# A modulation vector of 48 columns computed in three places instead of one

## The chip, the cores and the metric

The kernel runs on one core of one Trainium2 chip. The metric is the device time of one execution in microseconds (us); of several runs the median is given. One core has five engines with a queue of instructions each: TensorE (PE in the profile, with its weight loads as PEld), VectorE (DVE), ScalarE (ACT), GpSimd (POOL) and SyncE (SP), which here issues most DMAs. An engine works its queue off in order and waits where an operand or a buffer is not ready.

## The reference, cut to what matters

The input x has 512 tokens of 1024 features. It passes two blocks with different weights. The change lies in the second, whose norms and residual sums are modulated by a vector c of 1024 elements:

```python
c_act = jax.nn.silu(c)
mod = (c_act @ w_mod[l] + b_mod[l])[:, None, :]          # w_mod: 1024 x 6144
sh1, sc1, g1, sh2, sc2, g2 = jnp.split(mod, N_MOD, axis=-1)

h = _rms(x, norm1_w[l]) * (1 + sc1) + sh1
proj = h @ w_in[l]
...                                                      # S5 branch, sliding-window attention
x = x + g1 * (mixed @ w_out[l])

h2 = _rms(x, norm2_w[l]) * (1 + sc2) + sh2
x = x + g2 * _conv_ffn(h2, w_up[l], conv_w[l], conv_b[l], w_down[l])
```

The product with w_mod is one row by a matrix of 25 MB in fp32; its 6144 results are held as `modT`, 48 columns of 128 partitions. Columns 0 to 7 are the shift and 8 to 15 the scale of the first norm, 16 to 23 the gate g1, 24 to 31 and 32 to 39 shift and scale of the second norm, 40 to 47 the gate g2.

## The kernel before, in words

Feature tiles of 128 partitions by 512 tokens are the unit of work. In the trace the stages follow one another: block 1 (projections, three kinds of attention, a convolution, an output projection) to about 318 us, its feed-forward stage ("first feed-forward stage", weights w3 and w4) to about 722 us, the second block (S5 state space branch, sliding-window attention, gated linear unit, output projection) to about 955 us, and the "second feed-forward stage" (w8 and w9) to the end.

Weights come as pieces of 128x1024 fp32 (512 KB) over one queue, `_Lazy`: SP loads a piece into `raw` (L353; NRAW = 2 buffers), ACT rounds it to `whi` (L365), DVE or, for w6 to w8, POOL forms the rest `wlo` (L367), and PE multiplies with both parts (helper `mm`, L259). A `raw` buffer comes free when `wlo` is formed. One piece is prepared ahead of the one in use (AHEAD = 1).

In the feed-forward stages PE's products go to banks of `acc`; DVE empties them (`fg` L1299 and `fu` L1302 for the hidden tiles, `x` L1323 for the sum), which frees the bank for PE. Two generators of second-block work are interleaved with the first feed-forward stage: `s5_tables` and `modulation` (L1052). The function `fill()` (L1225) steps each generator once after every finished tile of that stage. `modulation` holds silu(c), spread over all partitions, in `cb`, and computes each of the 48 columns in two halves: SP loads 128x512 of w_mod into `wm` (three buffers, 256 KB), and one DVE instruction (L1061) multiplies it with `cb` and sums along the row. Whatever is left of the generators is run before the second block's first norm. The column groups of `modT` are read by `modulated` (both norms, through `a1`), `gm` (g1) and `down2` (g2, L1705).

ACT's functions come in table sets; a function outside the loaded set needs an ACT_TABLE_LOAD ahead of it. `tables()` at L306 loads a set by name that holds both the logarithm and the exponential, since `rsqrt_` (L497) writes every inverse square root as exp(-0.5 ln). In block 1 the head norms use it: `nss` (sums of squares on DVE), `nr` by L498 and L499 on ACT, a Newton step on DVE, `tokn`, and PE's transposes of `tokn`.

The order of PE's instructions in the second block is written out by hand in the string ORDER (a name and a number for each step: s, t and v are the three parts of the attention of one tile, g the gated unit, p the output products of the S5 branch, qp and qt projections and transposes of the queries, R and A norms). Elsewhere, and on the other engines everywhere, a scheduler sets the order at build time by its own estimate of when operands are ready; code that is written earlier and depends on little may be moved far ahead.

Of the kernel before, what the change touches and what calls it, by code (L numbers as in the profile page):

```python
# [17 lines left out]
P = 128  # L18
# [20 lines left out]
B2 = 1  # L39
# [6 lines left out]
ORDER = "U kp0 kp1 a0 a1 kt0 b0 qp0 c0 a2 b1 qp1 kt1 b2 c1 d0 a3 c2 qt0 qt1 b3 c3 d1 s0 qp2 s1 s2 t0 d2 t1 d3 e0 s3 e1 qt2 t2 s4 qp3 v0 t3 s5 v1 g0 qt3 g1 g2 t4 g3 s6 v2 v3 s7 t5 R p0 p1 v4 p2 t6 v5 p3 p4 v6 t7 p5 v7 p6 p7 A"  # L46
# [17 lines left out]
# ------------------------------------------------------------------ layout  # L64
# [29 lines left out]
def w_plan():  # L94
    """name -> list of (input, row0, n_k, columns): one contiguous [128, n_k * n] block each."""
# [29 lines left out]
def pvec(i):  # L125
    """per-partition vectors, name -> [128, n]"""
# [17 lines left out]
    o["b_mod"] = _fv(z(i["b_mod_2"])[0])  # L144
    o["sinks"] = _bc(z(i["sinks_2"])[0])
# [17 lines left out]
def consts():  # L163
    """constants of the shapes alone, name -> [128, n]"""
# [36 lines left out]
def arrays_of(i):  # L201
# [15 lines left out]
    a["wmod"] = np.ascontiguousarray(g("w_mod_2")[0].T).reshape(48, P, D)  # L217
    br, bi = (g(f"ssm_b_{n}_2")[0].transpose(1, 0, 2).reshape(64, 512) for n in ("re", "im"))
# [11 lines left out]
# ------------------------------------------------------------------ kernel  # L230
def build(tc, I, out, PV, PVN, CS, CSN, CS1, CSN1):
# [52 lines left out]
    # ---- constants and per-partition vectors  # L284
# [18 lines left out]
    def tables(after=None, name="natural_log_exp_and_others"):  # L303
        """activation tables that the next functions share"""
# [8 lines left out]
    # ---- weights: load, split into two 12-bit parts whose sum is the weight  # L313
# [10 lines left out]
    def cut(name, j):  # L324
        """block j as pieces: (first k, last k, first column, last column) each, with its source"""
# [11 lines left out]
    class _Lazy:  # L337
# [80 lines left out]
    for name, n in ( ("w2", 4), (("w3", "w4"), 0), ("w5", 5), ("w6", 2), ("w7", 8), (("w8", "w9"), 0)):  # L418
        if n == 0:
            enqueue_ffn(*name)  # L420
        for j in range(n):
# [21 lines left out]
    def proj_f(ps, w, x, m, k0=0, cs=ALL):  # L443
        """ps[m-feature, token] = W[:, m].T @ x"""
# [4 lines left out]
    def proj_group(group, x, order, cs=ALL):  # L449
        """several (ps, w, m) at once, the contraction outermost"""  # L450
# [6 lines left out]
    def proj_late(ws, x, early, late, done):  # L457
        """all 8 feature tiles; the first three wait for the late part of x last"""
# [13 lines left out]
    def proj_t(ps, w, x, t, n, o=0):  # L472
        """ps[token, o:o + n] = x[:, token].T @ W"""
# [13 lines left out]
    def split_scaled(dst, src, scale_col):  # L487
        """dst hi/lo of src * scale_col"""
# [7 lines left out]
    def rsqrt_(o, ms, scale=1.0):  # L496
        """o = (ms * scale + eps) ** -0.5, from the tables"""  # L497
# [3 lines left out]
    def rsqrt_m2(pool, tag, r, ms):  # L501
        """r = -2 * (ms + eps) ** -0.5, with a Newton step"""
# [6 lines left out]
    def head_norm(pool, wide, dsts, src, nh):  # L509
        """dsts[i][tok, heads, dup, 64] = -128 * src[tok, heads, 64] / rms, the heads in order"""  # L510
# [19 lines left out]
    # gains with the factors that the norms leave open: -1/128 per head norm, -1/2 per feature norm  # L530
# [12 lines left out]
    # ================================================================ block 1  # L543
# [6 lines left out]
    # ---- x, its squares, the unscaled normed input; the first products run along as the tiles of x come in  # L550
# [50 lines left out]
    # ---- bias tables of the causal attentions  # L601
# [11 lines left out]
    # compress chain inputs  # L613
# [11 lines left out]
    # ---- keys, values and gates of the sparse attention; queries and keys of all heads  # L625
# [15 lines left out]
    def kv_p(n):  # L641
        """two query tiles at a time"""
# [28 lines left out]
    def turn2(src):  # L671
        """both query tiles of a pair of heads side by side"""
# [6 lines left out]
    def kv_x(n):  # L679
        """hi and lo of the keys, the same on both halves of the partitions"""  # L680
# [12 lines left out]
    def qa_x(t):  # L693
        """the hi part of the queries on the lower half of the partitions, the lo part on the upper half"""
# [31 lines left out]
    # ---- compressed keys and values  # L726
# [65 lines left out]
    # ---- compressed branch, all tiles at once  # L792
# [28 lines left out]
    # ---- group norm of a finished feature tile, split for the next product  # L821
# [20 lines left out]
    # ---- softmax of one query tile, 4 heads  # L842
# [58 lines left out]
    # ---- stick-breaking: what is left of the stick before a key is the product of 1 - sigmoid over the later keys  # L901
# [32 lines left out]
    # ---- dilated  # L934
# [24 lines left out]
    # ---- short convolution  # L959
# [43 lines left out]
    def tok_norm(pool, parts, r, w="onesD", cs=ALL):  # L1003
        """-2 / rms of every token, on all partitions; the parts add up to the squares"""
# [26 lines left out]
    # ---------------------------------------------------------------- feed-forward 1, with work of block 2 beside it  # L1031
# [19 lines left out]
    def modulation():  # L1051
        cb = s5p.tile([P, D], F32, name="cb")  # L1052
        nc.sync.dma_start(cb, I["cbc"])
        act(cb, cb, AF.Silu)
        mh = s5p.tile([P, 2, 48], F32, name="mh")
        yield
        for j in range(48):
            for n in range(2):
                wm = s5p.tile([P, 512], F32, tag="wm", bufs=3, name="wm")
                nc.sync.dma_start(wm, I["wmod"][j][:, n * 512:(n + 1) * 512])  # L1060
                V.tensor_tensor_reduce(wm, wm, cb[:, n * 512:(n + 1) * 512], 1.0, 0.0, ALU.mult, ALU.add, mh[:, n, j:j + 1])  # L1061
            yield
        V.tensor_tensor(modT, mh[:, 0], mh[:, 1], op=ALU.add)
        V.tensor_tensor(modT, modT, V1("b_mod"), op=ALU.add)
        dbg("mod", modT)
        yield

    def s5_tables():
# [3 lines left out]
        def cmul(o_r, o_i, a_r, a_i, b_r, b_i, shape, E):  # L1072
            """o = a * b, complex; o may not overlap a or b"""
# [41 lines left out]
        # (a - 1) / lambda  # L1115
# [17 lines left out]
        # mag ** 8 and the rotations of 8, 16, .. 256 steps  # L1133
# [14 lines left out]
        for q in range(4):  # L1148
# [16 lines left out]
            # input to the state at the end of a chunk of 8 tokens  # L1165
# [17 lines left out]
            # state to output, powers 0..8  # L1183
# [11 lines left out]
            # within a chunk  # L1195
# [15 lines left out]
            # rotations of 0..63 chunks  # L1211
# [11 lines left out]
    fillers = [s5_tables(), modulation()]  # L1223
# [42 lines left out]
    def norm_tail(pool, tot, r, after, hold, before=None, TAIL=TAIL, NPOS=NPOS):  # L1266
        """the last feature tiles by halves of the tokens: the norm of one half runs beside the products of the other"""
# [42 lines left out]
    def sum_squares(tot, k, src, cs, sq):  # L1310
        """adds to tot, except for the last one, which is returned"""
# [36 lines left out]
    def start_u(cs):  # L1348
        if cs is HALVES[0]:
# [17 lines left out]
    # ================================================================ block 2  # L1367
# [373 lines left out]
```

## Time and profile before

| | |
|---|---|
| median of 3 runs | 1321.94 us (1320.47 to 1323.9) |
| the profiled execution's own time (span) | 1323.2 us |
| PE busy | 1247.0 us, 94% |
| DVE busy | 864.9 us, 65% |
| ACT busy | 501.5 us, 38% |
| POOL busy | 386.4 us, 29% |
| share of PE in the chain that ended last | 53% |
| share of DVE, of DMA | 16%, 8% |

The rows further down come from the profile of that one execution. Line numbers such as L1061 are those of the kernel before. The granted clock of TensorE (PEclk) is 1.00 at 2.4 GHz and 0.50 at 1.2 GHz; values between are means over a stretch.

### The profile page before, as it was taken

To read this page: it belongs to the slowest core of one execution; us is meant where nothing else is said; L and a number is where in the kernel's file an instruction comes from. 1 tells how busy PE (TensorE), PEld (TensorE's weight loads), DVE (VectorE), ACT (ScalarE), POOL (GpSimd) and SP (SyncE) were. 2 spreads that over 40 slices of the span, in tenths; PEclk is the share of its full clock that TensorE was granted. 3 is DMA by queue.
4 is the path that set the end of the run, shared out by engine and by line. 5 is a ranking of instruction groups with operands and counts; after the bars stand their busy time and mean duration, and the time that the engine had idled before them with its cause. 6 is when DMAs were issued, how large, how long until landed. Compare 5 with 4: busy or idle time off the path is not lost.

```text
span 1323.2 us, 17207 instructions
## 1 busy us (share of the span) xinstructions
PE 1247.0 (94%) x6269; PEld 1005.0 (76%) x6269; DVE 864.9 (65%) x1615; ACT 501.5 (38%) x862; POOL 386.4 (29%) x403
## 2 busy tenths in 40 slices
PE   7999999999979878999999989979899999999998
PEld 6888765667857657788888978757888888888887
DVE  7668768767988878745445778795855443435362
ACT  5334466445213122322233432663454333333330
POOL 3000004012327439092511143025152423232300
PEclk8999999999999999999999986779899999999999
DMA  5431111126567676643434763331132423232321
GB/s 213 140 123 49 50 32 49 51 77 197 160 198 252 196 248 200 187 147 111 145 109 156 268 175 116 80 96 58 39 99 84 135 85 107 82 108 82 105 87 63
DMA packets 163668, 164.11 MB, mean 124 GB/s; under 512 B 12160, under 2 KB 127760, under 8 KB 163584
## 3 DMA queue, kind: packets, MB, share of 16 engines
q1 hardware_dynamic: 154240, 146.43, 36.2%
q0 software_dynamic: 4256, 12.29, 3.0%
q10 hardware_dynamic: 5088, 4.29, 1.0%
q8 instruction: 49, 0.80, 0.3%
q14 instruction: 35, 0.29, 0.1%
HBM read 149.39 MB, written 15.43 MB: 125 GB/s over the span
## 4 chain that ended last, share of the span: by engine, by line
PE 53%; DVE 16%; DMA 8%; issue 4%; ACT 2%; POOL 0%; DVEq 0%; SPq 0%; ACTq 0%; POOLq 0%
PE acc L259 31%; PE sc L259 10%; PE tr L259 9%; DMA wm<-in_wmod_dram 6%; DVE wm L1061 3%; DMA raw<-in_w_dram 2%; DVE wlo L367 2%; PE po L259 1%; ACT whi L365 1%; DVE hd L494 1%; DVE z L1441 1%; DVE x L1655 1%; DVE z L1442 1%; PE tr L1591 0%; DVE sqsum L1317 0%
## 5 line engine op out<-in xcount | busy, mean ns | idle before, releaser
L259 PE MATMUL acc<-hl,whi 128*128 128x512 f32 (+1 forms) x1624 | 489.5, 385 | 20.9 <-DVE fg L1299 7.5
L259 PEld LDWEIGHTS acc<-hl,whi 128*128 128x128 f32 x1624 | 298.8, 192 | 90.3 <-issue 19.1
L365 ACT ACTIVATE whi<-raw 128x1024 fp32r<-128x1024 f32 (+1 forms) x187 | 193.9, 1039 | 378.4 <-PE acc L259 178.0
L259 PE MATMUL acc<-hl,wlo 128*128 128x512 f32 (+1 forms) x812 | 311.2, 383 | 0.0
L367 DVE TENSOR_TENSOR wlo<-raw,whi 128x1024 fp32r<-128x1024 f32 (+1 forms) x133 | 170.3, 1282 | 67.4 <-ACT whi L365 64.7
L367 POOL TENSOR_TENSOR wlo<-raw,whi 128x1024 fp32r<-128x1024 f32 x54 | 132.2, 2450 | 265.9 <-ACT whi L365 265.9
L259 PEld LDWEIGHTS acc<-hl,wlo 128*128 128x128 f32 x812 | 155.1, 191 | 32.3 <-issue 2.4
L259 PE MATMUL acc<-hd,whi 128*128 128x512 f32 (+1 forms) x472 | 146.4, 393 | 19.3 <-DVE fu L1302 9.2
L259 PEld LDWEIGHTS acc<-hd,whi 128*128 128x128 f32 x472 | 87.9, 191 | 42.7 <-issue 12.7
L259 PE MATMUL acc<-whi,hl 128*128 128x256 f32 (+1 forms) x544 | 111.2, 295 | 1.6 <-ACT tok L246 1.6
L1061 DVE CUSTOM_DVE_ANT_0 wm<-wm,cb 128x512 f32<-128x512 f32 x96 | 87.1, 929 | 30.3 <-DMA wm<-in_wmod_dram 29.3
L259 PEld LDWEIGHTS acc<-whi,hl 128*128 128x128 f32 x544 | 91.1, 199 | 6.2 <-ACT tok L246 3.0
L259 PE MATMUL acc<-hd,wlo 128*128 128x512 f32 (+1 forms) x236 | 92.5, 392 | 0.0
L259 PE MATMUL acc<-wlo,hl 128*128 128x256 f32 (+1 forms) x272 | 79.9, 294 | 0.5 <-DVE wlo L367 0.5
L259 PE MATMUL tr<-hl,whi 128*128 128x512 f32 (+1 forms) x240 | 72.8, 386 | 0.0
L259 PE MATMUL sc<-hl,whi 128*128 128x512 f32 x208 | 64.9, 393 | 0.0
L914 POOL TENSOR_SCALAR_AFFINE_SELECT keep<-keep 128x128 f32<-128x128 f32 x16 | 9.3, 595 | 185.2 <-ACT keep L908 184.4
L259 PEld LDWEIGHTS acc<-wlo,hl 128*128 128x128 f32 x272 | 54.3, 200 | 2.6 <-DVE wlo L367 1.0
L259 PEld LDWEIGHTS acc<-hd,wlo 128*128 128x128 f32 x236 | 45.3, 192 | 9.5
L259 PEld LDWEIGHTS tr<-hl,whi 128*128 128x128 f32 x240 | 44.5, 188 | 9.8
L1323 DVE TENSOR_TENSOR x<-x,acc 128x512 f32<-128x512 f32 (+1 forms) x49 | 31.9, 655 | 28.8 <-PE acc L259 28.7
L259 PE MATMUL tr<-hl,wlo 128*128 128x512 f32 (+1 forms) x120 | 46.3, 386 | 0.0
(422 smaller groups left out, 1963.8 us busy)
## 6 DMA issues: line engine op xcount, KB each, us to landing
raw<-in_w_dram SPq DMA_DIRECT2D x177, 512.0 KB, 4.3
wm<-in_wmod_dram SPq DMA_DIRECT2D x96, 256.0 KB, 3.9
xk<-in_xT_dram SPq DMA_DIRECT2D x16, 256.0 KB, 4.7
d_g<-s5g POOLq DMA_DIRECT2D x4, 576.0 KB, 4.3
gt<-d_g SPq DMA_DIRECT2D x4, 576.0 KB, 4.0
w1c<-in_w1k_dram SPq DMA_DIRECT2D x8, 256.0 KB, 5.7
w1c<-in_w1v_dram SPq DMA_DIRECT2D x8, 256.0 KB, 7.1
raw<-in_w_dram SPq DMA_DIRECT2D x8, 256.0 KB, 2.7
```

What stands on the lines that cost most here:

```text
L259: nc.tensor.matmul(o, lhsT=l, rhs=r, start=start, stop=stop, **k)
L365: act(hi[:, :m], raw[:, :m], AF.Copy)
L367: E.tensor_tensor(lo[:, :m], raw[:, :m], hi.bitcast(F32)[:, :m], op=ALU.subtract)
L494: V.tensor_tensor(dst[:, 1], src, dst.bitcast(F32)[:, 0], op=ALU.subtract)
L914: G.affine_select(g[:, d], g[:, d], fill=1.0, **past)
L1061: V.tensor_tensor_reduce(wm, wm, cb[:, n * 512:(n + 1) * 512], 1.0, 0.0, ALU.mult, ALU.add, mh[:, n, j:j + 1])
L1323: V.tensor_tensor(x[k][:, cs], x[k][:, cs], ps[:, cs], op=ALU.add)
L1441: V.scalar_tensor_tensor(dst[re], src[im], sign, t[im], op0=ALU.mult, op1=ALU.mult)
L1442: V.scalar_tensor_tensor(dst[im], src[re], -sign, t[re], op0=ALU.mult, op1=ALU.mult)
L1655: V.tensor_tensor(x[k][:, cs], x[k][:, cs], t[:, cs], op=ALU.add)
```

## The change

The 48 columns are computed in three places.

- Columns 0 to 23 stay in the first feed-forward stage, by the same DVE instruction. The generator takes two or three steps of `fill()` for a column (`wait`), where it took one.
- Columns 24 to 39 become sixteen steps m24 to m39 in ORDER, in the second block. Each loads 128x1024 of a re-ordered copy of w_mod, `wmodk`, through the weight queue into a `raw` buffer (`_ModPiece`), multiplies it in eight fp32 products of one column with silu(c) (`cT`, features on the partitions) into a bank of the `tr` pool, and DVE adds b_mod. The 16 pieces stand among those of w6 and w7 in the queue, in order of use.
- Columns 40 to 47 are computed by DVE in the second feed-forward stage, into a tile `modG`, stepped after each of its tiles.

`cT` is computed by one Silu on ACT from a column group of `pv`, which gets 8 more columns. The factors of the two norms (`norm_gain`) are formed separately, those of the second norm after m39. Docstrings and comments also go away.

```diff
+MOD1, MOD2 = 24, 40
-ORDER = "... s4 qp3 v0 t3 s5 v1 g0 qt3 g1 g2 t4 g3 s6 v2 v3 s7 t5 R p0 p1 v4 p2 t6 v5 p3 p4 v6 t7 p5 v7 p6 p7 A"
+ORDER = "... s4 qp3 m24 v0 m25 t3 m26 s5 v1 m27 g0 m28 qt3 m29 g1 m30 g2 m31 t4 g3 m32 s6 m33 v2 v3 m34 s7 t5 m35 R p0 m36 p1 v4 m37 p2 t6 m38 v5 p3 p4 m39 v6 t7 p5 v7 p6 p7 A"
...
+    class _ModPiece(_Lazy):
+        def fetch(self):
+            if self.raw is None:
+                self.raw = wpool.tile([P, WM], F32, tag="raw", bufs=NRAW, name="raw")
+                nc.sync.dma_start(self.raw[:, :D], I["wmodk"][self.j])
+        def load(self):
+            self.fetch()
+            self.parts = self.raw
...
-    def modulation():
+    def modulation(pool, j0, j1, dst, wait):
...
-            yield
+            for _ in range(wait(j)):
+                yield
...
+    act(cT, V1("c"), AF.Silu)
...
-    fillers = [s5_tables(), modulation()]
+    fillers = [s5_tables(), modulation(s5p, 0, MOD1, modT[:, :MOD1], lambda j: 2 + j % 2)]
...
+    def mod_p(j):
+        w = wpieces["mod", j].get()
+        ps = tr()
+        for k in range(KD):
+            mm(ps[:, :1], w[:, k * P:(k + 1) * P], cT[:, k:k + 1], k == 0, k == KD - 1)
+        V.tensor_tensor(modT[:, j:j + 1], ps[:, :1], V1("b_mod", j), op=ALU.add)
+        if j == MOD2 - 1:
+            norm_gain(1)
...
-        V.scalar_tensor_tensor(x[k], ps, modT[:, 40 + k:41 + k], x[k], op0=ALU.mult, op1=ALU.add)
+        V.scalar_tensor_tensor(x[k], ps, modG[:, k:k + 1], x[k], op0=ALU.mult, op1=ALU.add)
...
+    last8 = modulation(fp, MOD2, 48, modG, lambda j: j % 2)
-    ffn("w8", "w9", h2, hidden2, down2, start=started, banks=(tr, sc, acc) if B2 else (acc,))
+    ffn("w8", "w9", h2, hidden2, down2, lambda: next(last8, None), start=started, banks=(tr, sc, acc) if B2 else (acc,))
```

What this does to the order of instructions shows at three places. The first is ACT's queue at the start of block 1. The names: `hl` is a tile of x in two parts, `pv` the vectors, `nr` the inverse root of a head norm. Before, its first rows, and further down the first head norm:

```order
L306 ACT_TABLE_LOAD
L623 DMA w2c<-in_w2c_dram 128x256
L489 ACTIVATE hl<-xk,pv 128x512
...
L365 ACTIVATE whi<-raw 128x1024
L498 ACTIVATE nr<-nss,eps 128x4
L499 ACTIVATE nr<-nr 128x4
L246 ACTIVATE tok<-sc,r_tok 128x128
```

With the change, the same places on ACT:

```order
L309 ACT_TABLE_LOAD
L647 DMA w2c<-in_w2c_dram 128x256
L1097 ACT_TABLE_LOAD
L1097 ACTIVATE cT<-pv 128x8
L513 ACTIVATE hl<-xk,pv 128x512
...
L522 ACT_TABLE_LOAD
L522 ACTIVATE nr<-nss,eps 128x4
L523 ACT_TABLE_LOAD
L523 ACTIVATE nr<-nr 128x4
L249 ACTIVATE tok<-sc,r_tok 128x128
```

The Silu of `cT`, written at the start of the feed-forward stage, has moved to ACT's first work of the program, behind the load by name. From there to about 230 us of the trace the logarithm and the exponential of each norm of block 1 have a load each: the program has 45 ACT_TABLE_LOADs instead of 18, one for `cT` and 13 pairs more.

The second place is PE in the second block, behind the last projection of the queries (qp3). `po` is an attention output, `prob` the weights of it, `sc` the scores. Before:

```order
L259 MATMUL acc<-whi,hl 128x256
L259 MATMUL po<-pt,v_6746 64x2x128 x2
L1591 MATMUL tr<-cst,prob_7590 128x128 x8
L259 MATMUL sc<-k2T_6748,q2T_6751 128x256
L259 MATMUL sc<-k2T_6748,q2T_6752 128x256
```

With the change, the same place on PE:

```order
L262 MATMUL acc<-whi,hl 128x256
L262 MATMUL tr<-cT,raw 128x1 x8
L262 MATMUL po<-pt,v_6603 64x2x128 x2
L262 MATMUL tr<-cT,raw 128x1 x8
L1625 MATMUL tr<-cst,prob_7443 128x128 x8
L262 MATMUL tr<-cT,raw 128x1 x8
L262 MATMUL sc<-k2T_6605,q2T_6608 128x256
```

Sixteen such groups of eight products now stand in PE's order between the steps of the attention, the gated unit and the output products.

The third place is SP's queue in that part of the second block, where `x_4` to `x_7` are the residual tiles read back. Before:

```order
L1637 DMA x_3_8095<-d_x 128x512
L353 DMA raw<-in_w_dram 128x1024 x2
L1637 DMA x_4_8119<-d_x 128x512
L353 DMA raw<-in_w_dram 128x1024
L1637 DMA x_5_8156<-d_x 128x512
```

With the change, the same place on SP:

```order
L1681 DMA x_3_8132<-d_x 128x512
L381 DMA raw<-in_wmodk_dram 128x1024 x2
L356 DMA raw<-in_w_dram 128x1024
L381 DMA raw<-in_wmodk_dram 128x1024 x3
L356 DMA raw<-in_w_dram 128x1024
L1681 DMA x_4_8152<-d_x 128x512
L381 DMA raw<-in_wmodk_dram 128x1024
L1681 DMA x_5_8207<-d_x 128x512
```

The pieces of w6 and w7 now alternate with pieces of `wmodk`, all of them in the two `raw` buffers.

## Rows read from the trace of the kernel before

**Rows 1.** The page: busy time by engine, and the chain that ended last.

```profile
PE 1247.0 (94%) x6269; PEld 1005.0 (76%) x6269; DVE 864.9 (65%) x1615; ACT 501.5 (38%) x862; POOL 386.4 (29%) x403
...
PE 53%; DVE 16%; DMA 8%; issue 4%; ACT 2%; POOL 0%; DVEq 0%; SPq 0%; ACTq 0%; POOLq 0%
```

**Rows 2.** The page: groups (busy, mean ns | idle before), DMA issues (KB, us).

```profile
L365 ACT ACTIVATE whi<-raw 128x1024 fp32r<-128x1024 f32 (+1 forms) x187 | 193.9, 1039 | 378.4 <-PE acc L259 178.0
...
L367 POOL TENSOR_TENSOR wlo<-raw,whi 128x1024 fp32r<-128x1024 f32 x54 | 132.2, 2450 | 265.9 <-ACT whi L365 265.9
...
L1061 DVE CUSTOM_DVE_ANT_0 wm<-wm,cb 128x512 f32<-128x512 f32 x96 | 87.1, 929 | 30.3 <-DMA wm<-in_wmod_dram 29.3
...
raw<-in_w_dram SPq DMA_DIRECT2D x177, 512.0 KB, 4.3
```

**Rows 3.** Stretches: length, busy time of the engines, clock, DMA share, GB/s.

```profile
core 0: us, PE busy (x) PEld busy (x) DVE busy (x) ACT busy (x) POOL busy (x), PEclk, DMA share, GB/s
317.00:432.00 115.00, 104.57 (x450) 82.89 (x449) 100.95 (x256) 35.47 (x50) 49.82 (x61) 0.96 0.66 205
432.00:541.00 109.00, 92.15 (x386) 71.33 (x385) 88.94 (x143) 22.49 (x30) 58.05 (x74) 0.95 0.69 216
...
566.00:700.00 134.00, 134.00 (x610) 108.22 (x609) 65.71 (x74) 39.30 (x51) 57.19 (x108) 1.00 0.41 123
...
853.60:906.90 53.30, 44.53 (x211) 32.41 (x209) 42.38 (x85) 31.92 (x76) 18.36 (x9) 0.87 0.23 70
960.00:1300.00 340.00, 340.00 (x1511) 277.91 (x1510) 157.99 (x205) 125.59 (x158) 99.47 (x41) 1.00 0.32 95
```

**Rows 4.** Waits: PE's from 432 to 541, then one of DVE's, 300 to 722.

```profile
PE acc L259 <- DVE fg L1299: 8.8, 3, 4.0
PE acc L259 <- DVE x L1323: 5.7, 4, 2.7
...
DVE wm L1061 <- DMA wm<-in_wmod_dram: 29.3, 25, 3.0
```

**Rows 5.** Timeline of PE (start, us): fp32 products of 64 columns, of one.

```profile
829.86 0.39 PE L259 MATMUL acc<-sp,gt 128*128 128x64 f32 x2
...
831.20 0.39 PE L259 MATMUL acc<-sp,gt 128*128 128x64 f32 x2
...
794.08 0.63 PE L259 MATMUL acc<-ua,tt 128*128 128x64 f32 x2
...
799.63 0.64 PE L259 MATMUL acc<-sp,gt 128*128 128x64 f32 x2
...
25.85 1.33 PE L259 MATMUL tr<-cst,sqs 128*128 128x1 f32 x8
```

**Rows 6.** Stretches as in Rows 3, and PE's waits from 853.6 to 906.9.

```profile
794.00:813.40 19.40, 17.94 (x84) 17.38 (x84) 16.85 (x36) 3.05 (x8) 7.74 (x6) 0.50 0.27 85
828.70:831.50 2.80, 2.80 (x27) 2.80 (x27) 2.38 (x10) 2.76 (x4) 0.00 (x0) 1.00 0.00 0
...
860.00:884.00 24.00, 15.25 (x71) 11.14 (x69) 22.59 (x31) 14.16 (x27) 9.92 (x4) 0.84 0.41 121
...
PE sc L259 <- DVE ml L1573: 4.9, 1, 4.9
PE tr L1524 <- DVE pt L248: 3.8, 1, 3.8
```

**Rows 7.** Timeline of ACT: a change of table sets, two head norms; PE's transpose.

```profile
230.08 1.28 ACT L498 ACT_TABLE_LOAD   x1
231.37 0.69 ACT L498 ACTIVATE rg<-sc,eps 128x512 f32<-128x512 f32 x1
...
39.72 0.30 ACT L498 ACTIVATE nr<-nss,eps 128x4 f32<-128x4 f32 x1 [2.07 <-DVE nss L515]
...
43.55 0.29 ACT L498 ACTIVATE nr<-nss,eps 128x4 f32<-128x4 f32 x1
...
45.99 0.66 PE L676 MATMUL tr<-cst,tokn 128*128 128x128 f32 x4 [0.28 <-DVE tokn L526]
```

More of the change, by code (lines that the diff above doesn't have):

```diff
@@ L45 @@
 EN_AT = {'k1': (0, 4), 'v1': (4, 4), 'q1': (8, 12), 'h1': (20, 8), 'w1': (28, 8), 's1': (36, 8), 'o1': (44, 16), 't1': (60, 46), 'u2': (106, 4), 'z2': (110, 4), 'y2': (114, 4), 'k2': (118, 2), 'v2': (120, 2), 'q2': (122, 4), 'h2': (126, 12), 's2': (138, 12), 't2': (150, 14)}
-ORDER = "U kp0 kp1 a0 a1 kt0 b0 qp0 c0 a2 b1 qp1 kt1 b2 c1 d0 a3 c2 qt0 qt1 b3 c3 d1 s0 qp2 s1 s2 t0 d2 t1 d3 e0 s3 e1 qt2 t2 s4 qp3 v0 t3 s5 v1 g0 qt3 g1 g2 t4 g3 s6 v2 v3 s7 t5 R p0 p1 v4 p2 t6 v5 p3 p4 v6 t7 p5 v7 p6 p7 A"
+ORDER = "U kp0 kp1 a0 a1 kt0 b0 qp0 c0 a2 b1 qp1 kt1 b2 c1 d0 a3 c2 qt0 qt1 b3 c3 d1 s0 qp2 s1 s2 t0 d2 t1 d3 e0 s3 e1 qt2 t2 s4 qp3 m24 v0 m25 t3 m26 s5 v1 m27 g0 m28 qt3 m29 g1 m30 g2 m31 t4 g3 m32 s6 m33 v2 v3 m34 s7 t5 m35 R p0 m36 p1 v4 m37 p2 t6 m38 v5 p3 p4 m39 v6 t7 p5 v7 p6 p7 A"
+MOD1, MOD2 = 24, 40
 NW = 16
@@ L144, in pvec @@
     o["b_mod"] = _fv(z(i["b_mod_2"])[0])
+    o["c"] = _fv(z(i["c_2"])[0])
     o["sinks"] = _bc(z(i["sinks_2"])[0])
@@ L217, in arrays_of @@
     a["wmod"] = np.ascontiguousarray(g("w_mod_2")[0].T).reshape(48, P, D)
+    a["wmodk"] = np.ascontiguousarray(g("w_mod_2")[0].reshape(KD, P, 48, P).transpose(2, 1, 0, 3)).reshape(48, P, D)
     br, bi = (g(f"ssm_b_{n}_2")[0].transpose(1, 0, 2).reshape(64, 512) for n in ("re", "im"))
@@ L368, in load, with __init__ @@
             self.parts = v(hi), v(lo)
+    class _ModPiece(_Lazy):
+        def __init__(self, j):
+            self.j, self.raw, self.parts = j, None, None
+        def fetch(self):
[5 more added lines that the diff above has]
+            self.parts = self.raw
     wpieces, queue, limit = {}, [], [1 << 30]
@@ L417, in build @@
         enqueue(("w1", j))
-    for name, n in ( ("w2", 4), (("w3", "w4"), 0), ("w5", 5), ("w6", 2), ("w7", 8), (("w8", "w9"), 0)):
-        if n == 0:
+    for name, n in (("w2", 4), (("w3", "w4"), 0), ("w5", 5), (None, 0), ("w7", 8), (("w8", "w9"), 0)):
+        if name is None:
+            for step in ORDER.split():
+                if step[0] == "m":
+                    wpieces["mod", int(step[1:])] = p_ = _ModPiece(int(step[1:]))
+                    queue.append(p_)
+                elif step in ("g0", "g2", "p0", "p2", "p4", "p6"):
+                    enqueue(("w6" if step[0] == "g" else "w7", int(step[1:]) // 2))
+        elif n == 0:
             enqueue_ffn(*name)
-        for j in range(n):
+        for j in range(4 if name == "w7" else 0, n):
             enqueue((name, j))
@@ L1049, in build @@
     d_z = [dpool.tile([8, 16, 8, 64], F32, name=f"d_z{q}") for q in range(4)]
-    def modulation():
-        cb = s5p.tile([P, D], F32, name="cb")
+    cT = cpool.tile([P, KD], F32, name="cT")
+    modG = cpool.tile([P, 8], F32, name="modG")
+    def modulation(pool, j0, j1, dst, wait):
+        n_ = j1 - j0
+        cb = pool.tile([P, D], F32, name="cb")
         nc.sync.dma_start(cb, I["cbc"])
         act(cb, cb, AF.Silu)
-        mh = s5p.tile([P, 2, 48], F32, name="mh")
+        mh = pool.tile([P, 2, n_], F32, name="mh")
         yield
-        for j in range(48):
+        for j in range(n_):
             for n in range(2):
-                wm = s5p.tile([P, 512], F32, tag="wm", bufs=3, name="wm")
-                nc.sync.dma_start(wm, I["wmod"][j][:, n * 512:(n + 1) * 512])
+                wm = pool.tile([P, 512], F32, tag="wm", bufs=3, name="wm")
+                nc.sync.dma_start(wm, I["wmod"][j0 + j][:, n * 512:(n + 1) * 512])
                 V.tensor_tensor_reduce(wm, wm, cb[:, n * 512:(n + 1) * 512], 1.0, 0.0, ALU.mult, ALU.add, mh[:, n, j:j + 1])
-            yield
-        V.tensor_tensor(modT, mh[:, 0], mh[:, 1], op=ALU.add)
-        V.tensor_tensor(modT, modT, V1("b_mod"), op=ALU.add)
-        dbg("mod", modT)
+            for _ in range(wait(j)):
+                yield
+        V.tensor_tensor(dst, mh[:, 0], mh[:, 1], op=ALU.add)
+        V.tensor_tensor(dst, dst, V1("b_mod")[:, j0:j1], op=ALU.add)
         yield
+    act(cT, V1("c"), AF.Silu)
     def s5_tables():
@@ L1331, in build, with norm_gain @@
     a1 = cpool.tile([P, 16], F32, name="a1")
+    def norm_gain(n):
+        nm, o = (("norm1", 8), ("norm2", 32))[n]
+        V.tensor_scalar(a1[:, n * 8:n * 8 + 8], modT[:, o:o + 8], 1.0, -0.5, op0=ALU.add, op1=ALU.mult)
+        V.tensor_tensor(a1[:, n * 8:n * 8 + 8], a1[:, n * 8:n * 8 + 8], V1(nm), op=ALU.mult)
     def modulated(n, r, dst, cs, tmp):
@@ L1352, in start_u @@
                     pass
-            for n, (nm, o) in enumerate((("norm1", 8), ("norm2", 32))):
-                V.tensor_scalar(a1[:, n * 8:n * 8 + 8], modT[:, o:o + 8], 1.0, -0.5, op0=ALU.add, op1=ALU.mult)
-                V.tensor_tensor(a1[:, n * 8:n * 8 + 8], a1[:, n * 8:n * 8 + 8], V1(nm), op=ALU.mult)
+            norm_gain(0)
         with tc.high_priority():
```

2 lines of the change are left out of this document (1 added, 1 removed).

## The prediction

> **What bounds the kernel now.** I read the page first: PE is busy 94% of the span and holds 53% of the chain that ended last [rows 1]. So the time is PE's work plus the few stretches in which PE waits, and every part of the change has two questions: does it take a PE wait away, and does it put work or a wait on PE. The costliest group that the change touches is next: 96 reductions of `wm` on DVE, 929 ns each, 87.1 us, with 30.3 us of idle time before them, nearly all for the transfer of `wm` [rows 2]. DVE's busy time is no cost by itself; it costs where PE waits for DVE.
>
> The table of stretches tells where that is [rows 3]. From 566 to 700 us, when no reduction is left, PE is busy all of 134.00 us with 610 products, at clock 1.00: 0.2197 us a product. From 432 to 541, where the last half of the reductions runs, 386 products take 109.0 us; at the later rate they need 84.8. **24 us are lost there.** From 317 to 432, 450 products take 115.0 us and need 98.9, so 16 us are lost; some of that is the norm at the start of the stage and the S5 tables. DVE is busy 89 of the 109 us, and the waits of PE say how it reaches PE [rows 4]: `acc` banks that DVE has not emptied, `fg` 8.8 us and `x` 5.7 us. In DVE's own list stand 29.3 us in 25 waits for `wm` [rows 4]: a reduction without its data holds up the emptying of banks behind it. The rest of the loss is the clock: 0.95 and 0.96 in these stretches, 1.00 later [rows 3].
>
> In the second block, from 853.6 to 906.9 (where m24 to m39 will stand), PE is busy 44.5 of 53.3 us [rows 3], and two waits for DVE make 8.7 us [rows 6]. So this stretch has little room: whatever PE work beyond some 9 us is put there lengthens it.
>
> **The first feed-forward stage.** It loses 48 reductions, 48 x 0.929 = 44.6 us of DVE, with 12 MB of transfers. I take the whole loss of the later stretch as returned, **-24**. That assumes the 24 columns that stay sit in the first part, as SP's queue has it: their `wm` loads alternate with `raw` as densely as before, and end where half of them had ended. So the two or three steps of `fill()` for a column do not spread them, and the 16 us lost before 432 stay. The best case is that all 40 us return; the worst that DVE's other work (S5 tables) holds some of the waits and only the 14.5 us of waits in [rows 4] return. Range -40 to -15.
>
> **The sixteen steps on PE.** Eight fp32 products of 128x128 by 128x1 make a step. The trace has such products on 64 columns, where one product shows as two passes (x2) [rows 5]: 829.86 to 831.20 holds six pairs of passes, 0.223 us a pair, 111 ns a pass; 794.08 to 799.63 holds 13 pairs, 0.427 us each, 213 ns a pass. The granted clock in the two stretches is 1.00 and 0.50 [rows 6], 2.4 and 1.2 GHz. With one column alone there is a row too: eight passes of `tr<-cst,sqs` take 1.33 us, 166 ns a pass [rows 5], between the two. Few columns do not make a pass cheap; the 128x128 weights do the work. A step is 16 passes: 1.78 us at full clock, 3.41 at half; sixteen steps 28.5 or 54.6 us. Of this at most the 8.7 us of waits can be absorbed, so 20 us is the floor.
>
> The buffers come on top. A piece of `wmodk` needs 4.3 us of transfer [rows 2] and holds its `raw` buffer until PE has done the step; a piece of w6 or w7 holds one for 4.3 + 1.04 (ACT) + 2.45 (POOL) = 7.8 us. There are two buffers, 16 pieces of the one kind and six of the other in 53.3 us; with 1.78 us of use the buffer time is 16 x 6.1 + 6 x 7.8 = 144 us, 72 us at two buffers, more than the stretch has, near the 53.3 + 28.5 = 82 us that it would get. I followed ORDER piece by piece with these durations and PE at full clock: the stretch becomes 84 us, +31. The waits for a piece then lower the clock: it is 0.87 as a mean before and 0.84 from 860 to 884 [rows 3, 6]. Half of the steps at 1.2 GHz add 8 x 1.63 = 13 us, and better use of the present waits takes about 6 away. I take **+38**, range +20 (floor) to +60 (all at half clock, and 5 us of waits). DVE gets 16 sums of one column behind its softmax work; it is busy 22.6 of 24 us there [rows 6], so a `tr` bank comes free late, which is in the range. SP's queue holds the residual tiles `x_4` to `x_7` behind these pieces; they are needed late, which I cost at nothing because the products of w7 that they join come later still; if a piece waits for a buffer, so do they.
>
> **The Silu of `cT` in block 1.** The instruction is small, but the scheduler has moved it to the start of ACT's queue, behind the load of the set that holds ln and exp together. The rows of the order show the result: 27 more table loads, 26 of them as pairs around the logarithm and exponential of block 1's norms. A load takes 1.28 us, and the next function starts at its end (230.08 + 1.28, `rg` at 231.37) [rows 7]. All 26 on the path would be 33.4 us. A load has no operand to wait for, so the first of a pair runs while ACT waits for the sums: at 39.72 ACT had been idle 2.07 us, which hides it; at 43.55 it had not been idle at all, which does not [rows 7]. The second of a pair always lies between ln and exp. What hides that is PE having other products. At 45.99 PE is already waiting, 0.28 us, for the normed `tokn` [rows 7]. Of the 13 pairs seven have a transpose behind them within 0.3 us or already waited for; the others have microseconds to spare. Five at one load and two at two are 9 x 1.28 = 11.5: **+11**. The range is +3 (PE's other products cover most) to +20.
>
> *The rule beside it.* The Trainium skill, "ScalarE: Activation LUTs", section "What ACT_TABLE_LOAD costs", gives 1283 ns for the load, as the trace does, and some 1380 ns of drain with it, 2.66 us per switch. By that figure nine loads would cost 24 us instead of 11.5. The trace disagrees: between the start of the load and the start of `rg` lie 1.29 us [rows 7].
>
> **The second feed-forward stage.** 16 reductions, 16 x 0.929 = 14.9 us of DVE, and 4 MB. PE is busy all 340 us of its main stretch, DVE 158 of them [rows 3], so 15 us more fit into DVE's idle half. **+1**, range 0 to +4 (two or three late banks as in [rows 4], at clock loss). The cover is DVE's idle half; it is gone only if `wm` is late.
>
> **The sum.** -24 + 38 + 11 + 1 = +26. On the profiled execution, 1323.2 us, this gives 1349.2; that execution is 1.3 us above the median, so 1348 us on the median.
>
> **Rivals.**
> *Faster.* PE's waits absorb all they can, the pieces are always there, and the first stage gives back all of its loss. The place is the attention of the second block, and the point from which it decides is whether buffers feed a step each 4.6 us (82 us of stretch less the waits, over 16). -40 + 20 + 3 + 0 = -17, about 1305. For it: DMA is busy for a share of 0.23 there [rows 3]. Against: 22 pieces through 2 buffers. 9%.
> *Cheap passes.* Suppose products of one column are nearly free, their weight loads hidden behind the products before. Then a piece holds its buffer for the transfer and little more: 16 x 4.3 + 6 x 7.8 = 116 us, 58 at two buffers, 5 more than the stretch has; pieces do not come evenly, so I take twice that, +10. -24 + 10 + 11 + 1 = -2, about 1320. The rows at 64 columns and at one column speak against it, 111 and 166 ns a pass [rows 5]. 6%. The Trainium skill, "TensorE: Matmul & The Clock Gate", section "Back-to-back issue gap", states about 25 ns as the floor of a product of 1 to 64 columns; 256 passes would be 6.4 us by it, where the rows give 28.5 at least.
> *Half clock.* The waits in the attention keep PE at 1.2 GHz through all sixteen steps: +60 for that part, 1322 - 24 + 60 + 11 + 1 = 1370. For it: clock 0.50 for 19.4 us on end with hardly a wait [rows 6]. Against: 0.87 as a mean of the very stretch [rows 3]. 15%.
> *Costlier switches.* Where each load also empties ACT, or delays the softmax behind it, block 1 pays double: 1322 - 24 + 38 + 22 + 1 = 1359. 15%.
> *The change does not relieve the first stage.* The 24 columns stand as densely as ever, and the waits move with them: -15 instead of -24, and what the S5 tables hold stays: 1357. 5%.
>
> **How the numbers follow.** The forecast as summed has 50%. Half clock, costlier switches and no relief are also slower, so slower has 0.85. A measurement here tells about 0.3%, 4 us, from no change: cheap passes end within it, 0.06; the faster rival gives 0.09. The range of 8 in 10 leaves out the faster rival, part of the cheap passes, and the upper half of the half-clock case: 1322 to 1374.
>
> **What would show it.** In the profile after: from 432 to 541 of the first feed-forward stage, no wait of PE for `fg` or `x`, and the stage ends about 24 us earlier; `tr<-cT,raw` groups of 16 passes and 1.8 to 3.4 us each, with PE waits for `raw` before them, and the stretch from qp3 to v6 at some 90 us; ACT_TABLE_LOAD rows at the lines of `rsqrt_`, and PE waits for `tokn` of more than 1 us in block 1, whose end moves by about 11 us. The prediction is wrong if the passes are hidden (groups under 1 us), if block 1 ends where it did, or if PE in the first stage stays as slow.

## The result, and the profile after

The changed kernel takes 1371.88 us (median of 4 runs, 1366.58 to 1377.4); the kernel before took 1321.2 us beside it. The ratio is 1.0374, with a 95% interval of 1.034 to 1.0408. The profiled execution has a span of 1367.6 us, 44.4 more than before.

Where the 44 us arose is read from four marks that both programs have: the first and the last `fg` on DVE (start and nearly the end of the first feed-forward stage), and the first and a late `cf` on ACT (second feed-forward stage). The first fence is the timeline of the kernel before, the second that of the changed kernel; the first column is the start in us.

```profile
326.34 0.69 DVE L1299 SCALAR_TENSOR_TENSOR fg<-acc,r 128x512 f32<-128x512 f32 x1
...
679.03 0.69 DVE L1299 SCALAR_TENSOR_TENSOR fg<-acc,r 128x512 f32<-128x512 f32 x1 [2.29 <-PE acc L259]
...
968.73 1.45 ACT L1692 ACTIVATE cf<-acc,pv 128x512 f32<-128x512 f32 x2 [4.28 <-PE acc L259]
...
1279.11 0.63 ACT L1701 ACTIVATE cf<-cf 128x512 f32<-128x512 f32 x1 [2.72 <-DVE cf L1694]
```

```profile
350.50 0.68 DVE L1330 SCALAR_TENSOR_TENSOR fg<-acc,r 128x512 f32<-128x512 f32 x1
...
680.44 0.69 DVE L1330 SCALAR_TENSOR_TENSOR fg<-acc,r 128x512 f32<-128x512 f32 x1 [2.31 <-PE acc L262]
...
1013.34 0.78 ACT L1736 ACTIVATE cf<-acc,pv 128x512 f32<-128x512 f32 x1 [0.63 <-PE acc L262]
...
1323.67 0.63 ACT L1745 ACTIVATE cf<-cf 128x512 f32<-128x512 f32 x1 [2.72 <-DVE cf L1738]
```

Differences of neighbouring marks give the four parts: block 1 +24.2, the first feed-forward stage -22.8 (24.2 to 1.4), the second block +43.2 (1.4 to 44.6), the second feed-forward stage 0.0 (44.6 to 44.6).

The stretches of the changed kernel that answer to [rows 3], with the same columns:

```profile
core 0: us, PE busy (x) PEld busy (x) DVE busy (x) ACT busy (x) POOL busy (x), PEclk, DMA share, GB/s
341.00:456.00 115.00, 107.21 (x456) 84.40 (x455) 99.84 (x251) 34.62 (x48) 48.71 (x64) 0.96 0.65 201
456.00:565.00 109.00, 106.15 (x474) 85.75 (x473) 67.72 (x79) 31.88 (x41) 51.20 (x73) 0.98 0.46 138
565.00:700.00 135.00, 135.00 (x615) 109.09 (x614) 65.33 (x74) 40.00 (x51) 59.90 (x109) 1.00 0.41 125
852.10:948.40 96.30, 89.78 (x464) 73.55 (x462) 40.63 (x101) 32.56 (x76) 19.08 (x10) 0.73 0.37 121
1005.00:1345.00 340.00, 340.00 (x1509) 277.79 (x1508) 178.59 (x241) 127.07 (x160) 99.59 (x41) 1.00 0.37 107
```

*First feed-forward stage.* In its second stretch of 109 us PE now does 474 products instead of 386 [rows 3], nearly the rate of the third. One wait of PE is left from 456 to 565, 2.8 us for `fu`, where [rows 4] has 8.8 us for `fg` and 5.7 us for `x`. The first stretch is as slow as it was: 456 products in 115 us, 450 before.

*Second block.* The part from the end of qp3 to v6 took 53.3 us [rows 3] and takes 96.3. PE is busy 45.3 us longer, and idle 2.3 us less. Ahead of this part the changed kernel gains 2.9 us, and behind it, up to the first `cf`, it loses 3.1. The products of m24 to m39 and their waits, some of the steps, and PE's three longest waits from 852 us to the first `cf`:

```profile
L262 PE MATMUL tr<-cT,raw 128*128 128x1 f32 x256 | 36.1, 271 | 3.5 <-DVE pt L251 2.4 <-ACT pt L249 1.0
...
852.11 1.84 PE L262 MATMUL tr<-cT,raw 128*128 128x1 f32 x16
...
858.31 3.57 PE L262 MATMUL tr<-cT,raw 128*128 128x1 f32 x16 [0.97 <-ACT pt L249]
...
865.73 3.57 PE L262 MATMUL tr<-cT,raw 128*128 128x1 f32 x16
...
912.61 3.57 PE L262 MATMUL tr<-cT,raw 128*128 128x1 f32 x16 [2.39 <-DVE pt L251]
...
PE acc L262 <- DVE xa L1698: 4.5, 3, 1.7
PE acc L262 <- ACT hl L1377: 3.4, 1, 3.4
PE acc L262 <- POOL wlo L370: 3.0, 2, 1.6
```

So 36.1 us are the passes themselves, 1.84 us a step at full clock and 3.57 at half (the three steps shown; the other thirteen took 1.84 to 2.25). No wait is for a piece of `wmodk`. The other 9 us of PE time are old products at a lower clock: the mean of the stretch is 0.73, where it was 0.87 [rows 3], and the products of the gated unit and of w7, as many as before, take longer each. First before, then changed:

```profile
L259 PE MATMUL acc<-hl,whi 128*128 128x512 f32 x72 | 25.1, 432 | 0.0
L259 PE MATMUL acc<-hl,wlo 128*128 128x512 f32 x36 | 14.9, 414 | 0.0
...
L262 PE MATMUL acc<-hl,whi 128*128 128x512 f32 x72 | 31.3, 525 | 0.0
L262 PE MATMUL acc<-hl,wlo 128*128 128x512 f32 x36 | 18.6, 517 | 3.0 <-POOL wlo L370 3.0
```

*Block 1.* The page's counts hold: 45 table loads. How they lie on the path shows in the chain that ended last, in the order of time, here around the second head norm:

```profile
45.62 1.28 ACT L522
46.91 0.30 ACT nr L522
47.23 1.28 ACT L523
48.52 0.21 ACT nr L523
```

L522 and L523 without a tile are the loads ahead of the logarithm and of the exponential. The chain from 24 to 340 us by line, and some of PE's longest waits there:

```profile
by line: PE acc L262 39.8%; PE sc L262 13.8%; PE po L262 8.9%; PE tr L895 4.2%; issue 3.9%; ACT L523 3.7%; ACT whi L368 2.6%; ACT L522 2.0%; DVE tokn L550 1.5%; DVE wlo L370 1.5%; PE tr L950 1.4%; POOL keep L938 1.3%; PE tr L700 1.1%; DVE p
...
PE acc L262 <- ACT tok L249: 4.9, 4, 2.1
PE tr L721 <- DVE tokn L550: 4.1, 2, 2.4
...
PE sc L262 <- DVE rsq L530: 2.3, 1, 2.3
```

3.7% and 2.0% of 316 us are 11.7 and 6.3 us: nine loads ahead of exponentials and five ahead of logarithms lie on the chain, 18 us.

How the delay grows shows in ACT's own rows (`rg` is the inverse root of a group norm). The ninth head norm and the first group norm, before and then changed:

```profile
149.96 0.30 ACT L498 ACTIVATE nr<-nss,eps 128x8 f32<-128x8 f32 x1 [2.12 <-DVE nss L515]
150.29 0.21 ACT L499 ACTIVATE nr<-nr 128x8 f32<-128x8 f32 x1
189.72 0.69 ACT L498 ACTIVATE rg<-sc,eps 128x512 f32<-128x512 f32 x1 [1.63 <-PE sc L259]
190.44 0.63 ACT L499 ACTIVATE rg<-rg 128x512 f32<-128x512 f32 x1
...
165.38 0.30 ACT L522 ACTIVATE nr<-nss,eps 128x8 f32<-128x8 f32 x1 [0.82 <-DVE nss L539]
166.99 0.21 ACT L523 ACTIVATE nr<-nr 128x8 f32<-128x8 f32 x1
206.41 0.69 ACT L522 ACTIVATE rg<-sc,eps 128x512 f32<-128x512 f32 x1 [0.34 <-PE sc L262]
208.41 0.63 ACT L523 ACTIVATE rg<-rg 128x512 f32<-128x512 f32 x1
```

The load ahead of a logarithm runs in ACT's idle time: 2.12 us of it have become 0.82. The load ahead of an exponential adds 1.3 us, here from 15.4 to 16.7 us of delay, and 39 us later, with PE's other products between, the logarithm of the group norm is still 16.7 us late. Over all 13 pairs the exponentials add 17.1 us in this way, of which 2.9 are made up before the next logarithm; the rows up to and with the logarithms add 7.9, mostly where ACT had little or no idle time. The last 2.2 us come between the third group norm and the fourth, where PE's mean clock is 0.87 (228.5 to 254.3 us) and was 1.00 before (206.4 to 230.1); the delay is 24.2 us from there on.

### The profile page after: what moved, and what is told of

It is laid out like the page before. It is cut to its first block, busy times and chain, and to the rows that moved or that the text cites. A ratio compares the mean times of both kernels' runs of the same rounds, so it can differ in the third digit from the quotient of the medians.

```text
span 1367.6 us, 17632 instructions
## 1 busy us (share of the span) xinstructions
PE 1286.7 (94%) x6525; PEld 1041.0 (76%) x6525; DVE 838.7 (61%) x1569; ACT 538.0 (39%) x891; POOL 373.7 (27%) x403
## 4 chain that ended last, share of the span: by engine, by line
PE 70%; DVE 14%; ACT 6%; DMA 5%; issue 3%; POOL 2%; SPq 0%; DVEq 0%; ACTq 0%; POOLq 0%
PE acc L262 41%; PE sc L262 13%; PE tr L262 11%; DMA raw<-in_w_dram 3%; PE po L262 3%; DMA wm<-in_wmod_dram 2%; DVE wlo L370 2%; DVE wm L1090 1%; ACT whi L368 1%; PE tr L895 1%; ACT L523 1%; POOL sqs L597 1%; DVE x L1699 1%; POOL wlo L370 1%; DVE z L1476 1%
## 5 line engine op out<-in xcount | busy, mean ns | idle before, releaser
L1090 DVE CUSTOM_DVE_ANT_0 wm<-wm,cb 128x512 f32<-128x512 f32 x64 | 65.6, 1045 | 18.2 <-DMA wm<-in_wmod_dram 13.4
L262 PEld LDWEIGHTS acc<-hd,wlo 128*128 128x128 f32 x236 | 45.3, 192 | 9.6
```

What stands on the lines that cost most here:

```text
L262: nc.tensor.matmul(o, lhsT=l, rhs=r, start=start, stop=stop, **k)
```

## Experiments

**One part alone: the early Silu.**

```diff
+    o["c"] = _fv(z(i["c_2"])[0])
...
+    cT = cpool.tile([P, KD], F32, name="cT")
+    act(cT, V1("c"), AF.Silu)
     def modulation():        # kernel before, otherwise unchanged
```

> The kernel before with one part of the change alone: the Silu of c into cT, written where the change has it (the result is used by nothing). ACT's order shows 45 table loads, as with the change. Theory (the loads are the whole growth of block 1, 24 us in the two traces): 1321 + 24 = 1345 us, with block 1 ending at about 310 us instead of 286 (first residual sum x) and the rest as before. Rival 1 (the price of the prediction, nine loads on the path): 1332. Rival 2 (the growth comes from the other order of PE in block 1 that the change brings, not from the loads): under 1325.

Measured: 1343.94 us, ratio 1.0187 (1.0137 to 1.0237), 23 us more than the 1320.49 us of before beside it. The first `fg` stands at 354.35 us, 28.0 later than before:

```profile
354.35 0.69 DVE L1303 SCALAR_TENSOR_TENSOR fg<-acc,r 128x512 f32<-128x512 f32 x1
```

One activation of eight columns, whose result nobody reads, makes block 1 as long as the change does (by the last `fg`, at 703.07, the delay is 24.0 us). It also brings the changed kernel's order of PE in block 1, so this run doesn't tell the second rival from the loads. The traces of before and of the changed kernel do, for the greater part: the order differs only in the first 60 us, up to the transposes of the third head norm. Behind them the same product starts 5.9 us late, and the other 18.3 us of the 24.2 arise after it, with PE's products in the same order:

```profile
54.58 0.42 PE L259 MATMUL sc<-w1c,kkm 128*32 128x256 f32 x4
...
60.46 0.42 PE L262 MATMUL sc<-w1c,kkm 128*32 128x256 f32 x4
```

**The change without it.**

```diff
-    act(cT, V1("c"), AF.Silu)
...
-        act(cb, cb, AF.Silu)
+        s_ = act(cb, cb, AF.Silu)
+        if j0 == 0:
+            with tc.issue_after(s_.ins):
+                act(cT, V1("c"), AF.Silu)
```

> The changed kernel with the Silu of cT issued behind that of cb, in the first feed-forward stage: 18 table loads, as before. Theory (loads): 1372 - 24 = 1348 us, block 1 as before, all else as in the changed kernel. Rival (something else in block 1): above 1362.

Measured: 1348.98 us, ratio 1.023 (1.0187 to 1.0272): 23 us below the changed kernel. Block 1 is what it was before, by the first `fg` to a tenth of a us:

```profile
326.26 0.69 DVE L1331 SCALAR_TENSOR_TENSOR fg<-acc,r 128x512 f32<-128x512 f32 x1
```

Both experiments agree: block 1 grows by the early Silu, with the 27 table loads that it brings. How much of the first 5.9 us is the other order of PE stays open.

**Transfers without passes, passes without transfers, neither.** The first leaves seven of eight products out, the second gives all sixteen steps one small tile, loaded once, and the third does both.

```diff
-        for k in range(KD):
-            mm(ps[:, :1], w[:, k * P:(k + 1) * P], cT[:, k:k + 1], k == 0, k == KD - 1)
+        mm(ps[:, :1], w[:, :P], cT[:, :1], True, True)
```

> The changed kernel with one product of the eight in each of m24 to m39 (the other seven are left out, so the modulation is incomplete); all transfers of wmodk and the use of the raw buffers stay. Theory (PE's passes are the cost of the second block, 36 us of 46, and the low clock beside them): 7/8 of 36 go, -31, and up to 12 us of clock: 1329 to 1341 us. Rival (buffers and transfers hold PE up): above 1360, with PE waits for raw.

Measured: 1345.74 us, 26 less than the changed kernel. From the last `fg` to the first `cf` the trace takes 307.4 us, where before took 289.7 and the changed kernel 332.9: 17.7 us of the growth stay. PE now waits for the pieces of w6 and w7, from 681 to 989 us:

```profile
PE acc L262 <- ACT whi L368: 7.5, 4, 2.4
PE acc L262 <- POOL wlo L370: 6.3, 4, 2.2
...
L262 PE MATMUL tr<-cT,raw 128*128 128x1 f32 x32 | 5.5, 242 | 5.5 <-DVE pt L251 3.1 <-ACT pt L249 1.2 <-DMA raw<-in_wmodk_dram 1.0
```

With few passes the pieces come late: 13.8 us of waits for weight pieces, 12.0 of them between m24 and m39 where the changed kernel has 3.0, and 1.0 us for a piece of `wmodk` itself. The expectation of 1329 to 1341 missed that.

```diff
-                self.raw = wpool.tile([P, WM], F32, tag="raw", bufs=NRAW, name="raw")
-                nc.sync.dma_start(self.raw[:, :D], I["wmodk"][self.j])
+                modw.append(bp.tile([P, 384], F32, name="modw"))       # once
+                nc.sync.dma_start(modw[1], I["wmodk"][self.j][:, :384])
...
+            mm(ps[:, :1], w[:, k % 3 * P:k % 3 * P + P], cT[:, k:k + 1], k == 0, k == KD - 1)
```

> The changed kernel with all eight products of each of m24 to m39, but on one small tile loaded once (15 of the 16 transfers and the use of the raw buffers are left out, and the products use wrong weights). Theory (PE's passes): the second block keeps its length but for the late pieces of w6 and w7, some 5 us: 1363 to 1372 us. Rival (buffers): 30 us less, about 1342.

Measured: 1359.82 us, 12 less than the changed kernel by the medians and 3 below the range expected. In the trace the same stretch takes 328.7 us, 4.2 less; but the profiled execution took 1367.57 us, 7.8 more than the median of the four. So the passes alone keep 31 to 39 of the 43.2 us:

```profile
L262 PE MATMUL tr<-cT,modw 128*128 128x1 f32 x256 | 38.6, 280 | 5.3 <-ACT pt L249 3.0 <-DVE pt L251 2.4
```

> The changed kernel with both cuts in m24 to m39: one product of the eight, and on the small tile that is loaded once (seven products and 15 transfers of each sixteen are left out). With passes alone cut the second block still grew by 18 us, with transfers alone cut by 42. Theory (PE's passes and the raw buffers together are its whole growth of 46 us; either hides part of the other): 1372 - 46 + 4 (16 products, and sums on DVE) = 1330 us. Rival (DVE's 16 sums and the tr banks that wait for them hold some of it): 1340 or more.

Measured: 1336.5 us (1331.67 at the least), ratio to before 1.0093 (1.0062 to 1.0124), above the 1330 expected and below the rival's 1340. The stretch takes 296.4 us, 6.7 more than before. The products that are left, and two of PE's waits from 845 to 990 us, which only the sums into `modT` make:

```profile
L262 PE MATMUL tr<-cT,modw 128*128 128x1 f32 x32 | 6.0, 256 | 7.3 <-DVE pt L251 2.8 <-ACT pt L249 2.8 <-DVE modT L1670 1.7
...
PE tr L262 <- DVE modT L1670: 1.7, 1, 1.7
PE tr L1629 <- DVE modT L1670: 1.4, 1, 1.4
```

So some 7 us stay with one product a step: the 16 products left take 6.0 us of PE, and 3.1 us are waits for the `tr` bank behind a sum on DVE. The four kernels give each price twice, by the medians: seven products of eight cost 26 us with the transfers and 23 without them; the transfers cost 12 with the products and 9 without. The passes are the greater part either way. Whether the two hide part of each other, as this experiment expected, isn't shown: by the traces the transfers cost 4.2 us with the passes and 11.0 without, but the first figure comes from the one execution named above.

The mean clock from m24 to m39 goes with the passes, not with the waits for pieces. It is 0.74 with 256 passes and hardly a transfer, where PE waits for no piece there, and 0.83 with 32 passes and all transfers (0.81 with neither):

```profile
857.60:950.90 93.30, 87.95 (x466) 73.09 (x466) 44.90 (x104) 34.43 (x78) 19.48 (x10) 0.74 0.14 40
...
851.10:922.90 71.80, 53.20 (x242) 38.25 (x240) 40.44 (x101) 32.86 (x76) 17.62 (x9) 0.83 0.52 161
```

**24 columns alone in the first stage.**

```diff
-        for j in range(48):
+        V.memset(mh, 0.0)
+        for j in range(24):          # kernel before, columns 24 to 47 left out
```

> The kernel before with only columns 0 to 23 of the modulation (24 to 47 are left out and set to zero), everything else as before. Theory (the first feed-forward stage loses 24 to 26 us to the second half of the reductions and nothing else of the change acts on it): 1321 - 25 = 1296 us, with no PE wait for fg or x in the stretch after the last reduction. Rival (the waits come from the S5 tables as much): 1306 or more.

Measured: 1297.9 us, ratio 0.983 (0.9796 to 0.9863), 21 us less than the 1318.88 of before. In the trace the last `fg` comes 23.6 us earlier. What the first stage returns is worth what the prediction said, by itself.

**40 and 8, nothing on PE; then the same spread; then all 48 spread.** The first has before's ORDER and no `cT`; columns 40 to 47 go to the second feed-forward stage.

```diff
-    fillers = [s5_tables(), modulation(s5p, 0, MOD1, modT[:, :MOD1], lambda j: 2 + j % 2)]     # MOD1 = 24
+    fillers = [s5_tables(), modulation(s5p, 0, MOD1, modT[:, :MOD1], lambda j: 1)]             # MOD1 = 40
```

> The changed kernel without the products in the second block and without cT: columns 0 to 39 by DVE in the first feed-forward stage, 40 to 47 by DVE in the second. Theory (each column that leaves the first stage gives back about 1 us, and eight cost nothing in the second): 1321 - 8 = 1313 us. Rival (what is lost in the first stage is not in proportion, or the second stage pays): 1321 or more.

Measured: 1312.6 us, ratio 0.9948 (0.9925 to 0.9971), 6 us less than the 1318.88 of before.

```diff
-    fillers = [..., lambda j: 1)]
+    fillers = [..., lambda j: 1 + j % 2)]
...
+        i_ = V.tensor_tensor(u, u, t, op=ALU.mult)            # in hidden1; the same with x in down1
+        behind[0] = i_.ins
...
+                with tc.issue_after(behind[0]):
                     V.tensor_tensor_reduce(wm, wm, cb[:, n * 512:(n + 1) * 512], 1.0, 0.0, ALU.mult, ALU.add, mh[:, n, j:j + 1])
```

> The kernel of 40 and 8 columns with each pair of reductions in the first feed-forward stage ordered behind DVE's last instruction of the tile just finished (one pair after every one or two tiles, to the end of the stage), where the scheduler had packed them into its first two thirds. Theory (the loss comes from reductions standing densely ahead of the emptying of banks, and from their late data; after 566 us DVE is only half busy): the stage gives back 20 to 35 us, 1286 to 1301 us. Rival (a reduction ahead of every emptying makes PE wait at each tile): 1321 or more.

Measured: 1288.51 us, ratio 0.9753 (0.9721 to 0.9784). It beats both kernels, by 30 us and by 83. Two stretches, and PE's longest wait from 317 to 700 us:

```profile
317.00:432.00 115.00, 111.79 (x489) 89.11 (x488) 94.14 (x209) 37.06 (x53) 55.41 (x75) 0.99 0.52 162
432.00:541.00 109.00, 109.00 (x493) 88.46 (x493) 82.03 (x122) 33.26 (x42) 58.27 (x86) 1.00 0.65 197
...
PE acc L262 <- DVE x L1356: 2.4, 1, 2.4
```

[rows 3] and [rows 4] are the rows to lay beside it: with 40 of the 48 columns still there, from 432 to 541 PE is busy all of 109.00 us with 493 products instead of 386, the clock is 1.00, and the wait for `fg` is gone. DVE is hardly less busy, 82.0 us for 88.9. The reductions still wait for their data, 16.4 us in 11 waits; but no longer with a full `acc` bank behind them. The pace of the reductions and their place behind DVE's last instruction of a tile were changed together; which of the two does more isn't told apart.

> All 48 columns by DVE in the first feed-forward stage, as in the kernel before, spread over its tiles in the same way, nothing in the second block or the second feed-forward stage. Theory (density, not the number): 1290 to 1305 us. Rival (the number of reductions decides): 1315 or more, the same as the kernel before.

```diff
-MOD1, MOD2 = 40, 40
+MOD1, MOD2 = 48, 48
...
-    ffn("w8", "w9", h2, hidden2, down2, lambda: next(last8, None), ...)
+    ffn("w8", "w9", h2, hidden2, down2, ...)
```

Measured: 1293.65 us, ratio 0.978 (0.9739 to 0.9821). All the reductions of the kernel before, elsewhere in DVE's order, are worth 25 us (the pace is one or two steps of `fill()` for a column here too). Whether moving eight of them to the second stage adds to that isn't told apart: the ranges, 1285.5 to 1293.8 and 1285.9 to 1289.6, overlap.

**The change mended in two places.** The late Silu and the spread 24 columns together, with m24 to m39 as they are.

> The changed kernel with the Silu of cT behind that of cb, and the 24 columns of the first feed-forward stage spread over its tiles in place of its first third. The second block and the second feed-forward stage are as in the changed kernel. Theory (spreading returns the 12 to 16 us that the first third loses, and the second block still pays its 46): 1349 - 14 = 1335 us, slower than before. Rival (with 24 columns the first third loses to the S5 tables alone): 1345 or more.

Measured: 1335.62 us, ratio 1.0099 (1.006 to 1.0138). The first stage gives 13 us more, as expected: its last `fg` stands at 645.1 us, with 40 and 48 columns spread at 646.2 and 648.1. Unspread it stands at 655.4, 672.3 and 679.0 with 24, 40 and 48 columns. So the number of reductions counts where they are dense, and hardly where they are spread. The kernel as a whole is still slower than before: the second block's 43.6 us in its trace aren't to be had back by mending the rest.

## Why the prediction was right or wrong

The direction and the range (1322 to 1374) held; the time of 1348 us was 24 us too low. That the range held is partly luck: its upper end was set for half clock in the second block, and the measured time came near it by block 1, whose term lay outside its own range. By the prediction's terms, with the trace's figure behind each:

- **First feed-forward stage, -24: right, -22.8.** The columns that stayed sit in the first part, as the order of SP's queue had it; the losses of the first stretch stayed with them. 24 columns alone gave 23.6 us in the trace. The reason was right too (banks that DVE empties late), and the spread kernels show more than the prediction claimed: nearly the same comes back with all 48 columns left in the stage, if they are spread.
- **Sixteen steps on PE, +38: nearly, +43.2.** The passes were priced by the rows at 64 columns at 111 and 213 ns; they took 115 (1.84 us by 16) and 223 (3.57 by 16). The prediction put half of the steps at half clock, 41.5 us of passes in all; it was three of sixteen, and 36.1 us. In its place came something that had no term: the old products of the stretch ran slower, some 9 us, at a mean clock of 0.73 instead of 0.87. So half clock was counted for the new work and not for the old work beside it. The reason given for the lower clock, waits for pieces, wasn't borne out: no step waited for its piece, though such waits were named as a sign, the waits for `wlo` are 3.0 us, and the clock is as low where no piece is waited for (0.74). The size is nearly right in part because these two errors go against each other.
- **The Silu of `cT`, +11: the term that was mis-sized, +24.2, outside its range of +3 to +20.** A load did cost what the row said, and the first load of a pair was hidden by ACT's idle time, where there was any, as the prediction had it. What failed is "What hides that is PE having other products", said of the second load, by which six of the 13 pairs cost nothing and five of the rest one load each. In the trace the second load of every pair adds 1.3 us or somewhat more, and only ahead of the first and the ninth head norm is about one load made up again. So 14 loads lie on the chain, 18 us, instead of nine; of the 24.2 us the exponentials keep 14.2, the rows up to the logarithms add 7.9, and 2.2 come with the lower clock behind the third group norm. The three group norms alone carry the delay from 16.7 to 22.1 us, and the fourth starts 24.2 late.
- **Second feed-forward stage, +1: 0.0.** PE is busy all of 340.00 us there, with DVE at 178.6 instead of 158.0 [rows 3].

Of the rivals, *costlier switches* named nearly the time of block 1 (+22). Its first reading, that a load also empties ACT, fell: the load at 45.62 ends at 46.90 and `nr` starts at 46.91, so a switch costs 1.29 us, as in [rows 7]; 14 of them count instead of nine. The figure of the Trainium skill, "ScalarE: Activation LUTs", section "What ACT_TABLE_LOAD costs", 2.66 us with its drain, isn't seen here either. The second reading of this rival, that a load delays what stands behind it, is nearer to the rows, with the next norm in the place of the softmax. *Cheap passes* fell: one column took what 64 did. *Half clock* was so of three steps (858.31, 865.73 and 912.61, 3.57 us each) and of old products between them. *The change does not relieve the first stage* fell: -22.8, not -15; that the first third stays as slow was part of the forecast itself. *Faster* fell with the 43.2 us of the second block.

The sum of the terms as measured, 24.2 - 22.8 + 43.2 + 0.0 = 44.6, agrees with the difference of the spans, 44.4. The medians lie 50.7 apart: the profiled run of the kernel before lies 2.7 us above the median of its four, and that of the changed kernel 2.6 below.

## What to carry to other kernels

A small activation from another table set, put early by a scheduler, can undo a set that was loaded by name for a whole stage: count the table loads of the changed order, and let idle time of the engine hide only those ahead of a wait; a load between two activations that depend on each other went into the time here almost every time. Work that fills gaps on an engine should be ordered behind that engine's duties to the bottleneck, one piece after each; the 48 columns at their old cost were worth 25 us by this alone, and moving them to PE was worth less than nothing. On a bottleneck engine, price an fp32 product with one column like one with 64 (115 and 111 ns a pass here, at granted clock 1.00 and with new 128x128 weights for each product), and count the clock that its neighbours lose.

## What had not been expected of the hardware

- Eight fp32 products of 128x128 by 128x1, 16 passes, take 1.84 us at granted clock 1.00 and 3.57 at 0.50. Of three steps at half clock two follow a wait of PE (0.97 and 2.39 us) and one follows none (865.73); the mean clock of the stretch is 0.73.
- With the set that has both functions no longer loaded, the logarithm and the exponential of one norm each bring a load of 1.28 us: 26 loads for 13 norms.
- A reduction of 128x512 takes 0.68 or 0.69 us in most cases and up to 4.3 us in others, for a reason that no run here shows: in the second feed-forward stage of the changed kernel sixteen took 21.0 us, where 16 at the mean of [rows 2] would be 14.9. The stage got no longer by it.
